# The first chunk's weight blocks of an MLP's down projection, placed and loaded in another order

## The chip, the core and the metric

The kernel runs on one core of a Trainium2 chip. The metric is the device time of one execution in microseconds (us); the time of a kernel is the median of its runs.

## The reference, cut to what matters

A trunk of two encoder layers on one sequence of 1024 rows of 1024 floats. Each layer mixes the rows (Fourier mixing, attention, a convolution), and then an MLP follows, whose second half is what the change touches:

```python
D_MODEL, SEQ, DEPTH, D_FF = 1024, 1024, 2, 4096
for l in range(DEPTH):
    ...                                        # token mixing, layer norm
    h = jnp.square(jax.nn.relu(x @ w_ff1[l]))  # 1024 x 4096
    x = layer_norm(ALPHA * x + h @ w_ff2[l], ln2_g[l], ln2_b[l])
```

## The kernel before

**Arithmetic.** All is float32. TensorE multiplies a float32 matrix as a high and a low part: `split` (lines 167 to 169) lets ScalarE (ACT) write the high part (L168) and VectorE (DVE) or GpSimd (POOL) the rest (L169), and `mm3` (L173 to L176) issues three matmuls, high by high (L174), high by low (L175) and low by high (L176). Both operands have to be split before.

**Seven products.** Both matrix products of the MLP are made by seven block products in place of eight (the scheme of Strassen and Winograd), so blocks of the weights and of the activations are added and subtracted before they are split. In `ff`, 16 pairs of columns of `w_ff1` go through the seven products one after the other, and the seven combinations of hidden activations that the second product needs go to DRAM as `h_scratch`.

**Down projection.** `ff_down` works through 4 chunks of the 4096 hidden columns, each with seven products in the order `DOWN = (1, 2, 6, 5, 3, 7, 4)`: 28 steps. Step i has one of three places for its operands: A, the activations, loaded from `h_scratch` and split by `down_a` (L1403 to L1410: ACT the high part, POOL and VectorE the low one), and W, the weights, split by `prepare2`. Places 0 and 2 have A in a tile `w` and W in `T`; place 1 has both in `T`. A chunk needs four 1 MB blocks of `w_ff2`, called 11, 12, 21 and 22. Product 1 takes block 11, product 2 block 21. Product 6, the third step, needs `d` = 22 - (12 - 11), made in two halves (tile `d`, one buffer, L1473), and product 5, the fourth, needs 12 - 11 (L1470). Products 3, 7 and 4 need 22, 22 - 12 and 21 - `d`.

**The start of the first chunk.** The last two of the 16 pairs load blocks 11 and 21 early into the freed row tiles `rw` (L1363 to L1367), and products 1 and 2 are split from there inside `ff` (L1382, L1388). Then `up.close()` gives these pools back, and `ff_down` loads the four blocks (11 and 21 for the second time) into four buffers of the tile `b`, in the order 11, 12, 22, 21 (L1451). Residual rows of x come through the four small tiles `raw` (`residual`, L1485).

**What sets the order.** The order on each engine is set by a scheduler when the program is built, which plays the program through with its own costs. Each engine runs its list in order. All DMAs are issued by SyncE (SP), one list, whose loads and stores go through one hardware queue (q1).

Of the kernel before, what the change touches and what calls it, by code (L numbers as in the profile page):

```python
# [15 lines left out]
F32 = mybir.dt.float32  # L16
F32R = mybir.dt.float32r
AF = mybir.ActivationFunctionType
OP = mybir.AluOpType
# [3 lines left out]
P = 128  # L23
S = 1024
D = 1024
NT = S // P
KT = D // P
# [22 lines left out]
PAIRS, CHUNK = DFF // (2 * P), 4  # L50
# [58 lines left out]
class Trunk:  # L109
# [879 lines left out]
    def ff(self, l, Wh, psum, last):  # L989
        nc, tc, a = self.nc, self.tc, self.a  # L990
        v, g, act = nc.vector, nc.gpsimd, nc.scalar
# [3 lines left out]
        w2 = a["w_ff2"][l].rearrange("(c j i p) (b n) -> c i b p j n", j=CHUNK, i=2, p=P, b=2)  # L995
# [3 lines left out]
        def operands():  # L999
            W = self.ws.tile([P, KT, 2, 256], F32R, tag="w", name="w", bufs=2)  # L1000
            return W.rearrange("p k i n -> p (k i n)").rearrange("p (q i n) -> p q i n", q=4, i=2)
# [9 lines left out]
        up = ExitStack()  # L1011
        E = up.enter_context(tc.tile_pool(name="sum", bufs=1, side="right", reuse_waits="tile"))
        E = E.tile([P, 3, 4, 2, 512], F32R, name="E")
        p1 = up.enter_context(tc.tile_pool(name="up", bufs=1, reuse_waits="tile"))

        B = {1: slots[0], 2: slots[2], 3: E[:, 0], 5: E[:, 1], 6: E[:, 2], 7: slots[1], 4: slots[3]}

        ahead = [{n: self.T[:, k + j, :, 0:512] for j, n in enumerate((1, 2))} for k in (2, 6)]

        def load_rows(pool, n):  # L1020
            rw = pool.tile([P, KT, 256], F32, tag="rw", name="rw", bufs=1)
            for h in range(0, KT, 4):
                self.dma(rw[:, h:h + 4], w1[:, h:h + 4, n * 256:(n + 1) * 256])
            return rw
# [5 lines left out]
        class Pair:  # L1030
            def __init__(me, pool, n):
                me.rw, me.ops = load_rows(pool, n), {}
# [51 lines left out]
        def product(o, n, ops, first):  # L1084
            for k in range(4):
                self.mm3(o, [ops[n][:, i, k * P:(k + 1) * P] for i in (0, 1)], [B[n][:, k, i] for i in (0, 1)],
                         first and k == 0, k == 3, True)
# [5 lines left out]
        with tc.tile_pool(name="zo", bufs=1, reuse_waits="tile") as zp:  # L1093
# [104 lines left out]
            def bank():  # L1198
                return acc.tile([P, 512], F32, tag="x", name="x", bufs=6)
# [23 lines left out]
        p2 = up.enter_context(tc.tile_pool(name="up2", bufs=1, reuse_waits="tile"))  # L1223
# [99 lines left out]
        coming = third.prepare()  # L1323
# [30 lines left out]
        for n in range(2, PAIRS):  # L1354
            final = n == PAIRS - 1
            if not final:
                following = Pair((p1, p2)[(n + 1) % 2], n + 1)
                coming = following.prepare()
            else:
                following, coming = None, iter(())  # L1360
                wa, wb = operands(), operands()
                places = [(wa, slots[0]), (slots[2], slots[1]), (wb, slots[3])]
            if n >= PAIRS - 2:  # L1363
                row = (p1, p2)[n % 2].tile([P, KT, 256], F32, tag="rw", name="rw", bufs=1)
                row = row.rearrange("p k n -> p (k n)").rearrange("p (j n) -> p j n", j=CHUNK)
                self.dma(row, w2[0, n - PAIRS + 2, 0])
                early = [row] if n == PAIRS - 2 else early + [row]  # L1367
            H, ops = Hidden(n), pair.ops
            X, Y, Z = bank(), bank(), bank()
            product(X, 1, ops, True)  # L1370
            H.done1(X)
            product(Y, 6, ops, True)
            H.done6(Y)
            product(Z, 5, ops, True)
            H.done5(Z)
            product(X, 2, ops, False)
            H.done2(X)
            next(coming, None)
            next(coming, None)
            if final:  # L1380
                self.down_a(places[0][0], 0, 1)
                self.split(places[0][1][:, :, 0], places[0][1][:, :, 1], early[0])  # L1382
            product(Y, 7, ops, False)
            H.done7(Y)
            next(coming, None)
            if final:
                self.down_a(places[1][0], 0, 2)
                self.split(places[1][1][:, :, 0], places[1][1][:, :, 1], early[1])  # L1388
            product(Z, 3, ops, False)
            H.done3(Z)  # L1390
            H.sums()
            next(coming, None)
            X = bank()
            product(X, 4, ops, True)
            H.done4(X)
            for _ in coming:
                pass
            pair = following
        up.close()
        return self.ff_down(l, places, w2, last)  # L1400


    def down_a(self, A, ch, n):  # L1403
# [7 lines left out]

    def ff_down(self, l, places, w2, last):
        nc, tc, a = self.nc, self.tc, self.a
        v, g, act = nc.vector, nc.gpsimd, nc.scalar
        keep = ExitStack()
# [3 lines left out]
        rows = [y.rearrange("p i n -> p (i n)") for y in x]  # L1421
# [15 lines left out]
        with ExitStack() as c:  # L1437
            acc = c.enter_context(tc.tile_pool(name="xq", bufs=1, space=PSUM, reuse_waits="tile"))
            p3 = c.enter_context(tc.tile_pool(name="down", bufs=1, reuse_waits="tile"))

            def quarter():
                q = p3.tile([P, 2, D], F32, tag="b", name="b", bufs=4)
                return q.rearrange("p i n -> p (i n)").rearrange("p (j n) -> p j n", j=CHUNK)

            def load(ch, *names):
                for k in names:
                    coming[k] = quarter()
                    self.dma(coming[k], w2[ch, k // 10 - 1, k % 10 - 1])

            blocks, coming = {}, {}  # L1450
            load(0, 11, 12, 22, 21)  # L1451
            blocks, coming = coming, {}
            R = {n: [p3.tile([P, 512], F32, name=f"r{n}{t}") for t in range(4)] for n in (1, 6, 5)}
            R.update({n: [x[t + h][:, j] for t in range(4)] for n, h, j in ((2, 0, 0), (3, 0, 1), (4, 4, 0), (7, 4, 1))})

            def sub(dst, x, y):
                v.tensor_tensor(dst, x, y, OP.subtract)  # L1457


            def prepare2(i):  # L1460
                nonlocal blocks, coming
                ch, n = i // 7, DOWN[i % 7]
                A, W = places[i % 3]
                self.down_a(A, ch, n)
                more = ch + 1 < PAIRS // CHUNK
                if n == 1:
                    load(ch, 22)
                    blocks, coming = coming, {}
                if n == 6:
                    sub(blocks[11], blocks[12], blocks[11])  # L1470
                    for h in (slice(0, 2), slice(2, 4)):
                        d = p3.tile([P, 2, 512], F32, tag="d", name="d", bufs=1)
                        sub(d, blocks[22][:, h], blocks[11][:, h])  # L1473
                        sub(blocks[21][:, h], blocks[21][:, h], d)
                        self.split(W[:, h, 0], W[:, h, 1], d)
                    return
                if n == 3 and more:
                    load(ch + 1, 11)
                if n == 7:
                    sub(blocks[12], blocks[22], blocks[12])  # L1480
                if n == 4 and more:
                    load(ch + 1, 21, 12)
                self.split(W[:, :, 0], W[:, :, 1], blocks[{1: 11, 2: 21, 5: 11, 3: 22, 7: 12, 4: 21}[n]])
# [5 lines left out]

            steps = 7 * PAIRS // CHUNK  # L1490
            prepare2(2)
            for i in range(steps):
                ch, n = i // 7, DOWN[i % 7]
                final = ch == steps // 7 - 1
                A, W = places[i % 3]
# [5 lines left out]
                for t in range(4):  # L1501
# [6 lines left out]
                    r = R[n][t]  # L1508
# [30 lines left out]
                if 3 <= i + 3 < steps:  # L1539
                    prepare2(i + 3)  # L1540
# [64 lines left out]
```

## Time and profile before

| | us |
|---|---|
| median of 3 runs | 2338.55 (2334.68 to 2340.46) |
| the profiled execution | 2349.58 |
| its span, first to last instruction | 2347.8 |
| TensorE busy | 2220.0 |
| VectorE busy | 1782.8 |
| ScalarE busy | 1076.9 |
| GpSimd busy | 792.8 |

Rows below come from the profiled execution; their times count from the start of the span. PE is TensorE, DVE VectorE, ACT ScalarE, POOL GpSimd, SPq the list of DMAs. In a timeline row the first number is the start, the second the duration, and what stands in square brackets is the engine's idle time before it and who ended it. The first layer's down projection starts at about 858 us, the second's at about 2014 us.

### The profile page before, as it was taken

The page shows a single profiled execution, that of the slowest core. Times are in us where ns is not written, and L with a number is a line of the kernel's source. Part 1 is how long each engine was busy: PE and PEld are TensorE (multiplying, and loading weights), DVE is VectorE, ACT ScalarE, POOL GpSimd, SP SyncE. Part 2 cuts the span into 40 slices and gives each one's busy share as a digit, 9 for nine tenths or more (in the row PEclk, how much of TensorE's full clock was granted, in tenths as well). Part 3 has the DMA queues.
Part 4 walks back from the last instruction along what each step waited for, and adds up shares of the span by engine and source line. Part 5 has one row for each costly group of instructions (what it writes and reads, how often), then busy time and mean ns, then how long its engine had stood idle before and what let it go on. Part 6 is the DMA issues. An engine that isn't in the chain of part 4 may idle for free. (4 is left out here: it accounts for less than half of the span.)

```text
span 2347.8 us, 31000 instructions
## 1 busy us (share of the span) xinstructions
PE 2220.0 (95%) x11212; PEld 1873.3 (80%) x11212; DVE 1782.8 (76%) x2494; ACT 1076.9 (46%) x1851; POOL 792.8 (34%) x540
## 2 busy tenths in 40 slices
PE   7999999998999999999989999999899999899997
PEld 6888887976777877888788898788678778688886
DVE  7687668978776757778957866787887777767699
ACT  3343767844333344333343447677443333434333
POOL 2361203016332333434514702110353323443353
PEclk9999999999999999999999999999999999999999
DMA  8444763043444476644223539621344444765433
GB/s 309 131 118 148 203 190 108 19 162 126 148 148 148 150 238 238 208 140 142 89 90 97 152 113 269 168 72 64 125 153 153 148 148 153 269 215 166 161 104 108
DMA packets 222854, 357.44 MB, mean 152 GB/s; under 512 B 21320, under 2 KB 100620, under 8 KB 221612
## 3 DMA queue, kind: packets, MB, share of 16 engines
q1 hardware_dynamic: 222700, 355.45, 46.7%
q8 instruction: 89, 1.46, 0.3%
q14 instruction: 65, 0.53, 0.1%
HBM read 244.44 MB, written 115.15 MB: 153 GB/s over the span
## 5 line engine op out<-in xcount | busy, mean ns | idle before, releaser
L174 PE MATMUL x<-T,w 128*128 128x512 f32 x1088 | 424.9, 393 | 21.1 <-ACT T L168 5.9
L175 PE MATMUL x<-T,w 128*128 128x512 f32 x1088 | 427.1, 393 | 7.5 <-DVE T L169 7.5
L176 PE MATMUL x<-T,w 128*128 128x512 f32 x1088 | 426.7, 393 | 5.2 <-POOL w L1409 2.6
L174 PEld LDWEIGHTS x<-T,w 128*128 128x128 f32 x1088 | 205.7, 189 | 69.4 <-issue 8.6
L175 PEld LDWEIGHTS x<-T,w 128*128 128x128 f32 x1088 | 206.6, 190 | 51.5 <-DVE T L169 8.6
L176 PEld LDWEIGHTS x<-T,w 128*128 128x128 f32 x1088 | 206.4, 190 | 50.3 <-POOL w L1409 4.1
L1409 POOL TENSOR_TENSOR w<-w 128x512 fp32r<-128x512 f32 x76 | 142.9, 1901 | 240.4 <-ACT w L1407 240.4
L169 POOL TENSOR_TENSOR w<-raw,w 128x512 fp32r<-128x512 f32 x96 | 138.0, 1462 | 239.2 <-ACT w L168 235.6
L169 POOL TENSOR_TENSOR w<-s,w 128x512 fp32r<-128x512 f32 x68 | 102.8, 1522 | 252.9 <-ACT w L168 199.6
L174 PE MATMUL x<-E,w 128*128 128x512 f32 x384 | 151.0, 393 | 4.6 <-ACT h L1266 4.6
L176 PE MATMUL x<-E,w 128*128 128x512 f32 x384 | 150.9, 394 | 2.0 <-POOL w L169 1.9
L175 PE MATMUL x<-E,w 128*128 128x512 f32 x384 | 150.6, 392 | 0.0
L174 PE MATMUL s<-w,T 128*128 128x256 f32 (+1 forms) x432 | 136.9, 318 | 7.4 <-ACT T L168 7.0
L168 ACT CAST T<-b 128x2048 fp32r<-128x2048 f32 x44 | 83.9, 1907 | 126.3 <-PE x L176 109.0
L169 DVE TENSOR_TENSOR T<-b,T 128x2048 fp32r<-128x2048 f32 x44 | 103.8, 2359 | 45.7 <-ACT T L168 45.7
L176 PE MATMUL s<-w,T 128*128 128x256 f32 (+1 forms) x432 | 135.5, 315 | 1.7 <-POOL T L169 1.2
L175 PE MATMUL s<-w,T 128*128 128x256 f32 (+1 forms) x432 | 135.1, 313 | 1.3 <-POOL w L169 1.3
L169 POOL TENSOR_TENSOR w<-rw,w 128x512 fp32r<-128x512 f32 x60 | 94.0, 1582 | 122.2 <-ACT w L168 122.2
L1044 DVE TENSOR_TENSOR s<-rw 128x512 f32<-128x512 f32 x62 | 52.1, 841 | 104.7 <-DMA rw<-in_w_ff_dram 101.0
L174 PE MATMUL x<-T 128*128 128x512 f32 x320 | 125.0, 391 | 0.0
L176 PE MATMUL x<-T 128*128 128x512 f32 x320 | 124.5, 389 | 0.0
L175 PE MATMUL x<-T 128*128 128x512 f32 x320 | 124.5, 389 | 0.0
(376 smaller groups left out, 5812.2 us busy)
## 6 DMA issues: line engine op xcount, KB each, us to landing
h_scratch<-h SPq DMA_DIRECT2D x224, 256.0 KB, 2.5
w<-h_scratch SPq DMA_DIRECT2D x38, 1024.0 KB, 5.4
rw<-in_w_ff_dram SPq DMA_DIRECT2D x64, 512.0 KB, 4.9
b<-in_w_ff_dram SPq DMA_DIRECT2D x32, 1024.0 KB, 6.2
raw<-x_scratch SPq DMA_DIRECT2D x72, 256.0 KB, 4.8
T<-h_scratch SPq DMA_DIRECT2D x18, 1024.0 KB, 5.2
raw<-in_w_in_dram SPq DMA_DIRECT2D x64, 256.0 KB, 3.4
x_scratch<-x SPq DMA_DIRECT2D x32, 256.0 KB, 6.2
```

The source lines that it names most:

```text
L168: self.nc.scalar.copy(hi, src)
L169: (lo_eng or self.nc.vector).tensor_tensor(lo, src, hi.bitcast(F32), OP.subtract)
L174: mm(out, l[0], r[0], start=first, stop=False, skip_group_check=more)
L175: mm(out, l[0], r[1], start=False, stop=False, skip_group_check=more)
L176: mm(out, l[1], r[0], start=False, stop=last, skip_group_check=more)
L1044: eng.tensor_tensor(quad(out), x, y, op)
L1409: nc.gpsimd.tensor_tensor(A[:, j, 1], f32[:, j], A[:, j, 0].bitcast(F32), OP.subtract)
```

## The change

The change keeps block 11 where it was loaded early: the tile `rw` moves to a pool of its own, `p0`, which stays open through `ff_down`. Within the last pair, once block 11 has been split for product 1, block 12 is loaded in four pieces of 256 KB through the tiles `raw`, and VectorE subtracts in place, so that the tile then holds 12 - 11. `ff_down` loads three blocks in place of four, in the order 22, 12, 21, into three buffers of `b`; in the later chunks block 11 goes to `p0`'s tile. In product 6 the split of `d` is written ahead of the subtraction 21 - `d`.

```diff
+        keep = ExitStack()
+        p0 = keep.enter_context(tc.tile_pool(name="rows", bufs=1, reuse_waits="tile"))
...
-            rw = pool.tile([P, KT, 256], F32, tag="rw", name="rw", bufs=1)
+            rw = (p0 if pool is p1 else pool).tile([P, KT, 256], F32, tag="rw", name="rw", bufs=1)
...
-                row = (p1, p2)[n % 2].tile([P, KT, 256], F32, tag="rw", name="rw", bufs=1)
+                row = (p0, p2)[n % 2].tile([P, KT, 256], F32, tag="rw", name="rw", bufs=1)
...
             H.done3(Z)
             H.sums()
+            if final:
+
+                b11 = early[0]
+                for j in range(CHUNK):
+                    r = self.raw().rearrange("p a n -> p (a n)")
+                    self.dma(r, w2[0, 0, 1, :, j])
+                    v.tensor_tensor(b11[:, j], r, b11[:, j], OP.subtract)
...
-            def quarter():
-                q = p3.tile([P, 2, D], F32, tag="b", name="b", bufs=4)
+            def quarter(k):
+                if k == 11:
+                    q = p0.tile([P, KT, 256], F32, tag="rw", name="rw", bufs=1).rearrange("p k n -> p (k n)")
+                    return q.rearrange("p (j n) -> p j n", j=CHUNK)
+                q = p3.tile([P, 2, D], F32, tag="b", name="b", bufs=3)
...
-            load(0, 11, 12, 22, 21)
-            blocks, coming = coming, {}
+            load(0, 22, 12, 21)
+            blocks, coming = {**coming, 11: b11}, {}
...
                 if n == 6:
-                    sub(blocks[11], blocks[12], blocks[11])
+                    if ch:
+                        sub(blocks[11], blocks[12], blocks[11])
                     for h in (slice(0, 2), slice(2, 4)):
                         d = p3.tile([P, 2, 512], F32, tag="d", name="d", bufs=1)
                         sub(d, blocks[22][:, h], blocks[11][:, h])
+                        self.split(W[:, h, 0], W[:, h, 1], d)
                         sub(blocks[21][:, h], blocks[21][:, h], d)
-                        self.split(W[:, h, 0], W[:, h, 1], d)
```

The scheduler puts the four pieces of block 12 near the start of the MLP, as soon as the `raw` tiles are free; before, the residual rows of the first four tiles stood there. On SP's list, from the load of product 1's activations to the blocks, before:

```order
L141 DMA w<-h_scratch 128x4x512
L141 DMA T<-h_scratch 128x4x512
L141 DMA h_scratch<-h 128x512
L141 DMA gb<-in_ln_g_dram 128x1024
L141 DMA h_scratch<-h 128x512
L141 DMA gb<-in_ln_b_dram 128x1024
L141 DMA w<-h_scratch 128x4x512
L141 DMA h_scratch<-h 128x512 x5
L141 DMA b<-in_w_ff_dram 128x4x512 x4
```

and after:

```order
L141 DMA w<-h_scratch 128x4x512
L141 DMA raw<-x_scratch 128x512 x4
L141 DMA T<-h_scratch 128x4x512
L141 DMA h_scratch<-h 128x512
L141 DMA gb<-in_ln_g_dram 128x1024
L141 DMA h_scratch<-h 128x512
L141 DMA gb<-in_ln_b_dram 128x1024
L141 DMA w<-h_scratch 128x4x512
L141 DMA h_scratch<-h 128x512 x5
L141 DMA b<-in_w_ff_dram 128x4x512 x3
```

Four loads of residual rows (256 KB each) now stand ahead of `T`, the activations of product 2, and three blocks stand where four stood.

On VectorE, for product 6 of the first chunk, before (`b_7826` is block 11, `b_7828` 12, `b_7830` 22, `d_7852` the first half of `d`, `T` the operand that is split):

```order
L1457 TENSOR_TENSOR b_7826<-b_7828,b_7826 128x2048
L1510 SCALAR_TENSOR_TENSOR x0_7802<-raw_7938,x_7925 128x512
L1510 SCALAR_TENSOR_TENSOR x1_7803<-raw_7954,x_7941 128x512
L1457 TENSOR_TENSOR d_7852<-b_7830,b_7826 128x1024
L1457 TENSOR_TENSOR b_7828<-b_7830,b_7828 128x2048
L169 TENSOR_TENSOR T_64<-b_7826,T_64 128x4x512
L1510 SCALAR_TENSOR_TENSOR x2_7804<-raw_7970,x_7957 128x512
L169 TENSOR_TENSOR T_64<-d_7852,T_64 128x2x512
```

and after (`rw_7513` holds 12 - 11, `b_7841` is 22, `b_7843` 12, `b_7845` 21):

```order
L1471 TENSOR_TENSOR d_7864<-b_7841,rw_7513 128x1024
L169 TENSOR_TENSOR T_64<-rw_7513,T_64 128x4x512
L1471 TENSOR_TENSOR b_7843<-b_7841,b_7843 128x2048
L1525 SCALAR_TENSOR_TENSOR x0_7817<-raw_7950,x_7937 128x512
L169 TENSOR_TENSOR T_64<-d_7864,T_64 128x2x512
L1525 SCALAR_TENSOR_TENSOR x1_7818<-raw_7966,x_7953 128x512
L1471 TENSOR_TENSOR b_7845<-b_7845,d_7864 128x1024
L1525 SCALAR_TENSOR_TENSOR x2_7819<-raw_7982,x_7969 128x512
L1525 SCALAR_TENSOR_TENSOR x3_7820<-raw_7998,x_7985 128x512
L1421 TENSOR_TENSOR w_7659<-w_7659 128x2x512
L1471 TENSOR_TENSOR d_7869<-b_7841,rw_7513 128x1024
```

The row of seven instructions up to the low part of `d`'s first half has become one of four ahead of it; the subtraction 12 - 11 is gone from here.

## Rows read from the trace of the kernel before

**Rows 1.** The page: busy time, share of the span and instructions of each engine.

```profile
PE 2220.0 (95%) x11212; PEld 1873.3 (80%) x11212; DVE 1782.8 (76%) x2494; ACT 1076.9 (46%) x1851; POOL 792.8 (34%) x540
```

**Rows 2.** Busy time by stretch: PE, PEld, DVE, ACT, POOL, granted clock, DMA, GB/s.

```profile
857.00:866.00 9.00, 7.12 (x23) 5.12 (x23) 7.94 (x8) 5.67 (x5) 7.22 (x4) 0.81 0.55 171
...
884.00:898.00 14.00, 8.13 (x26) 5.94 (x25) 14.00 (x10) 7.67 (x5) 7.00 (x3) 0.76 0.70 249
898.00:930.00 32.00, 32.00 (x143) 26.51 (x142) 19.64 (x15) 15.08 (x14) 9.47 (x6) 1.00 0.71 243
...
2038.00:2054.00 16.00, 8.50 (x23) 6.01 (x22) 16.00 (x12) 8.54 (x5) 7.45 (x4) 0.68 0.69 248
```

**Rows 3.** TensorE's waits on GpSimd, 855 to 900 us: total, times, longest.

```profile
PE x L176 <- POOL w L1409: 1.9, 2, 1.2
```

**Rows 4.** TensorE's timeline in the first layer, 884 to 897 us.

```profile
884.16 0.39 PE L176 MATMUL x<-T 128*128 128x512 f32 x1
886.55 1.20 PE L174 MATMUL x<-T,w 128*128 128x512 f32 x4 [2.00 <-ACT T L168]
891.61 0.80 PE L175 MATMUL x<-T,w 128*128 128x512 f32 x1 [3.87 <-DVE T L169]
...
896.55 0.39 PE L174 MATMUL x<-T,w 128*128 128x512 f32 x1
```

**Rows 5.** The same in the second layer, 2037 to 2054 us.

```profile
2037.95 0.39 PE L176 MATMUL x<-T 128*128 128x512 f32 x1
2042.22 1.44 PE L174 MATMUL x<-T,w 128*128 128x512 f32 x4 [3.87 <-ACT T L168]
2047.28 0.80 PE L175 MATMUL x<-T,w 128*128 128x512 f32 x1 [3.63 <-DVE T L169]
...
2053.57 0.39 PE L175 MATMUL x<-T,w 128*128 128x512 f32 x1
```

**Rows 6.** VectorE's timeline in the first layer, 880 to 902 us.

```profile
880.79 2.29 DVE L1457 TENSOR_TENSOR b<-b 128x2048 f32<-128x2048 f32 x1 [6.42 <-DMA b<-in_w_ff_dram]
...
889.74 0.68 DVE L1510 SCALAR_TENSOR_TENSOR x<-raw,x 128x512 f32<-128x512 f32 x1
890.33 1.22 DVE L169 TENSOR_TENSOR T<-d,T 128x1024 fp32r<-128x1024 f32 x1
...
899.22 2.30 DVE L1457 TENSOR_TENSOR d<-b 128x1024 f32<-128x1024 f32 x1
```

**Rows 7.** VectorE's timeline in the second layer, at the same place.

```profile
2036.46 2.29 DVE L1457 TENSOR_TENSOR b<-b 128x2048 f32<-128x2048 f32 x1 [7.64 <-DMA b<-in_w_ff_dram]
```

**Rows 8.** The four blocks, first layer: SP's timeline; time to landing (tile view).

```profile
871.87 2.96 SPq L141 DMA_DIRECT2D b<-in_w_ff_dram  x4
...
DMA to landing us min/median/max: 6.2/8.2/10.1
```

**Rows 9.** Issue of the activations of products 1 and 2, first layer.

```profile
847.94 0.37 SPq L141 DMA_DIRECT2D w<-h_scratch  x1
852.02 0.37 SPq L141 DMA_DIRECT2D T<-h_scratch  x1
```

**Rows 10.** ScalarE's high parts of activations, products 1 and 5, first layer.

```profile
856.04 1.91 ACT L1407 CAST w<-w 128x2048 fp32r<-128x2048 f32 x1 [7.51 <-DMA w<-h_scratch]
...
888.97 1.90 ACT L1407 CAST w<-w 128x2048 fp32r<-128x2048 f32 x1 [0.67 <-DMA w<-h_scratch]
```

**Rows 11.** GpSimd's low parts of activations, products 1, 2 and 5, first layer.

```profile
858.03 4.00 POOL L1409 TENSOR_TENSOR w<-w 128x512 fp32r<-128x512 f32 x2 [16.11 <-ACT w L1407]
862.78 5.49 POOL L1409 TENSOR_TENSOR T<-T 128x512 fp32r<-128x512 f32 x2 [0.75 <-ACT T L1407]
...
890.94 3.97 POOL L1409 TENSOR_TENSOR w<-w 128x512 fp32r<-128x512 f32 x2 [14.16 <-ACT w L1407]
```

**Rows 12.** VectorE before product 1's low part, first layer.

```profile
857.99 1.23 DVE L1410 TENSOR_TENSOR w<-w 128x1024 fp32r<-128x1024 f32 x1 [8.87 <-ACT w L1407]
```

**Rows 13.** Busy time, 848.5 to 852.5 us; columns as in rows 2.

```profile
848.50:852.50 4.00, 4.00 (x19) 3.31 (x18) 0.62 (x2) 0.04 (x1) 0.00 (x0) 1.00 1.06 395
```

More of the change, by code (lines that the diff above doesn't have):

```diff
@@ L1399, in ff @@
         up.close()
-        return self.ff_down(l, places, w2, last)
+        with keep:
+            return self.ff_down(l, places, w2, last, p0, b11)
     def down_a(self, A, ch, n):
@@ L1410, in down_a, with ff_down @@
         nc.vector.tensor_tensor(A[:, 2:4, 1], f32[:, 2:4], A[:, 2:4, 0].bitcast(F32), OP.subtract)
-    def ff_down(self, l, places, w2, last):
+    def ff_down(self, l, places, w2, last, p0, b11):
         nc, tc, a = self.nc, self.tc, self.a
@@ L1446, in load @@
                 for k in names:
-                    coming[k] = quarter()
+                    coming[k] = quarter(k)
                     self.dma(coming[k], w2[ch, k // 10 - 1, k % 10 - 1])
             blocks, coming = {}, {}
-            load(0, 11, 12, 22, 21)
-            blocks, coming = coming, {}
+            load(0, 22, 12, 21)
+            blocks, coming = {**coming, 11: b11}, {}
             R = {n: [p3.tile([P, 512], F32, name=f"r{n}{t}") for t in range(4)] for n in (1, 6, 5)}
```

## The prediction

> **What bounds the kernel now.** The page comes first: TensorE is busy for 2220.0 of 2347.8 us [rows 1], so only time in which TensorE stands still or runs slowly can be won. The busy time by stretch then shows where that is. In 898 to 930 us it starts 143 matmuls in 32 us, one in 0.224 us, at a granted clock of 1.00 (2.4 GHz). In 884 to 898 us it is busy for 8.13 of 14 us at a granted clock of 0.76, and in the second layer, 2038 to 2054 us, for 8.50 of 16 us at 0.68 [rows 2]. Both stretches are the start of product 6 in the first chunk, and the change works there.
>
> TensorE's timeline names the waits. In the first layer the last matmul of product 2 starts at 884.16, so the next could start at 884.4. It starts at 886.55, held by ScalarE's high part of `d`; four matmuls later it stands again until 891.61, held by VectorE's low part, and then runs 12 steps in 4.94 us, nearly twice as long as they should take [rows 4]. From 884.4 to 896.55 it has done 16 steps, 3.6 us at full rate, so 8.6 us are lost. In the second layer it is free at 2038.2 and has done 19 steps (4.3 us) by 2053.57: 11.1 us lost [rows 5]. **The two stalls together are 19.7 us**, and no more than that can come from them.
>
> The chain behind each wait is on VectorE. It waits 6.42 us for block 12, subtracts at 880.79, takes residual rows in, makes `d`, subtracts 22 - 12, splits product 5's weights, and only then, at 890.33, makes the low part of `d` [rows 6]. The second layer begins the same chain at 2036.46 [rows 7].
>
> **What the change removes and moves.** (1) *The blocks.* The four are issued from 871.87 on. The first lands 6.2 us later, at 878.1 [rows 8], the second at 880.8, where the subtraction starts [rows 6]: one block in 2.7 us, so a third at 883.5. The change puts 22 first and 12 second, and 12 - 11 is there already. So `d` can start at 878.1 in the first layer and at 2036.46 - 2.7 = 2033.8 in the second.
>
> (2) *VectorE up to the low part of `d`.* By the new row: `d` 1.2 (as the split of the same size at 890.33), the split of 12 - 11 2.3 and 22 - 12 2.3 (as the subtraction at 880.79), one residual 0.7, the low part of `d` 1.2 [rows 6]. First layer: 878.1 + 1.2 + 2.3 = 881.6, block 12 is there, 883.9, 884.6, 885.8. TensorE, free at 884.4, does three matmuls that need the high part alone, until 885.1, and waits 0.7 us. ScalarE's high part, 1 us behind `d`, is long done. Second layer: 2033.8 + 3.5 = 2037.3, then 2039.6, 2040.3, 2041.5; TensorE is there at 2038.9 and waits 2.6 us.
>
> (3) *VectorE up to the second half of `d`.* Behind that stand 1 residual (0.7), 21 - `d` (1.2), 2 residuals (1.4), the low part of product 5's activations, `d`'s second half, the split of 22, 21 - `d` and the split of `d`. The last five are 1.2 + 1.2 + 2.3 + 1.2 + 1.2 = 7.1 us if GpSimd is quiet, and 11.5 to 12 us if it is not: the same subtraction took 2.30 us at 899.22 [rows 6], beside GpSimd. So the low part of the second half is done 10.4 to 15.3 us after TensorE started again. TensorE has 21 + 24 + 4 matmuls until then, 11.0 us, so it waits 0 to 4.3 us. GpSimd works for 4 us on product 5's activations and later for 5.5 us on the next [rows 11], which leaves a gap between; I take 1.3 us in each layer.
>
> (4) *Product 5's activations* land behind three blocks, not four: 2.7 us before 888.97 [rows 10], 886.3. ScalarE needs 1.9 and GpSimd 4.0 us [rows 10, 11], so the two tiles that GpSimd makes are ready at 892.2. TensorE wants the second at 885.8 + 28 steps = 892.1. No wait, but nothing to spare.
>
> (5) *The clock.* In 857 to 866 us two waits of 1.9 us in all [rows 3] went with a granted clock of 0.81; 23 matmuls ran where 40 fit [rows 2], 3.8 us lost, so 1.9 beside the waits. For the 2.6 us of the second layer I charge the same 1.9 us (0 to 2.9, what that layer loses so now: 15 steps in 6.29 us, [rows 5]); for 0.7 us in the first nothing (0 to 1.9).
>
> (6) *Added.* Four subtractions of 128x512, 0.7 us each by the nearest row, stand on VectorE before product 1's low part, where it is idle for 8.87 us [rows 12]: nothing, as long as that part waits for ScalarE. The pieces of block 12 are loaded at the start of the MLP and have been there for hundreds of us. The four residual loads (1 MB) that stood there now leave at 850 to 852, as VectorE frees `raw`, on SP behind the load of product 1's activations (847.94) and ahead of `T` (852.02) [rows 9]. The queue is full there, DMA share 1.06 [rows 13], so `T` lands up to 2.7 us later. Its low part is made until 868.3 [rows 11] and product 2 starts 48 matmuls before 884.4, at 873.6: 5 us cover it. By 866 the share has fallen to 0.55 on average [rows 2], so the queue has caught up before the blocks. One block less (1 MB) and the second load of 11 go away.
>
> **The sum.** Left in the first layer: 0.7 + 1.3 = 2.0 of 8.6 us; in the second: 2.6 + 1.9 + 1.3 = 5.8 of 11.1. Won: 6.6 + 5.3 = 11.9 us. Against the profiled execution, 2349.6 us, that is 2337.7; the runs shown have their median 11 us lower, at 2338.55, and the stalls are the same program's, so 2338.55 - 11.9 = **2326.7**. With the bounds of (3) and (5) the win is 2.9 us (0.7 + 4.3 + 1.9 and 2.6 + 4.3 + 2.9 left) to 16.4 us (0.7 and 2.6 left).
>
> **The rivals.** *A: the stall only moves to the second half of `d`.* VectorE's row is a chain without a gap, and every subtraction in it that meets GpSimd takes twice as long: the bound of 2.9 us, 2335.6. For it speaks the 2.30 us row; against it that GpSimd is idle between its two jobs. The Trainium skill, "SBUF — State Buffer", Who interferes with whom, says that a VectorE instruction with two SBUF inputs contends with a GpSimd instruction that reads SBUF. The trace agrees (1.22 against 2.30 us for the same form).
>
> *B: the residual loads delay product 1.* If the DMA engines take the 1 MB in turns with product 1's activations, in flight from 847.94, these land 2.7 us after 856.04 [rows 10]; ScalarE, GpSimd (idle 16.11 us for it, [rows 11]) and TensorE all wait for that. Price: 2.7 us in both layers and 1.9 us of clock in the second, 7.3 us: 2334.0. Against it: the blocks landed one after the other, 2.7 us apart, which is a queue worked off in order. The Trainium skill, "DMA: Bandwidth & Descriptors", Queues, rings and completion order, says that completion is not first in, first out for one issuing engine. By that page B could happen; the landings of this trace show order. The same price holds if the queue has not caught up and the blocks come 2.7 us later.
>
> *C: slower.* In the buffer ring of three, the next chunk's block 12 takes the buffer of block 12, which is free only when product 7's weights are split; on SP's list product 4's activations stand behind this load. Products 3 and 7 give 96 matmuls, 21.5 us, of cover; two loads (5.4 us), landing, ScalarE and GpSimd (1.9 + 4.0) take some 13, so 8.5 us are to spare. If SP stood there for 20 us, each layer would lose 11.5 us: 23 - 11.9 = 11 us slower, 2349.6. It turns to slower from about 14.5 us on. Against it: product 7's split needs only product 6's last matmul, and that lies before the end of product 5 in the new row.
>
> *D: it does not do what it says*, the blocks or pieces not being where they should; the lists above exclude it, but for the 2.7 us counted under B.
>
> **How the numbers follow.** Forecast 0.68, A 0.14, B and D 0.12, C 0.04, and 0.02 for a gain above the bound. A measurement can tell some 0.3%, 7 us, from no change. The forecast's cases lie mostly above that (6 to 16 us), A and B below it: faster 0.67, same 0.28, slower 0.05. The range reaches from the best bound, 16.4 us, with 2 us for the spread of the runs (2334.68 to 2340.46), to A: 2320 to 2336.
>
> **What would show it.** In the profile after, block 22 should be subtracted at about 878 us, 6.2 us behind its issue; TensorE's waits at product 6 should be below 1 and 3 us, with the granted clock of that stretch near 1.00 in the first layer; a wait on VectorE's `T` some 11 us later tests (3); product 1's cast should still start at about 856 us, or B holds; and no wait may appear at product 4. The forecast is wrong if the second half's wait passes 3 us in both layers, or if the blocks land later behind the moved residual loads.

## The result and the profile after

The changed kernel takes 2328.55 us (median of 16 runs, 2322.37 to 2334.08), the kernel before beside it 2340.03 us (16 runs). The ratio is 0.9949, 95% interval 0.9937 to 0.9960: 12 us or half a per cent faster. The forecast was 2326.7 us.

The profiled execution has a span of 2326.3 us, 21.5 us less than the one before. That is more than the medians differ by, because the execution profiled before was 9.5 us above its median; the last paragraph on the prediction comes back to what of that is spread.

TensorE is busy nearly as long as it was (2217.1 us, 2220.0 before, [rows 1]), so that what changed is its idle time and its clock. First the busy times by engine, of the page:

```profile
PE 2217.1 (95%) x11212; PEld 1869.2 (80%) x11212; DVE 1776.1 (76%) x2500; ACT 1077.1 (46%) x1851; POOL 793.3 (34%) x540
```

The busy time by stretch (length; busy us and instructions of PE, PEld, DVE, ACT, POOL; granted clock; DMA share; GB/s) answers to [rows 2]: product 1 and the start of product 6 in the first layer, then the start of product 6 in the second.

```profile
853.00:862.00 9.00, 8.28 (x36) 6.34 (x35) 7.02 (x6) 6.71 (x5) 4.43 (x3) 1.00 0.95 330
880.00:886.00 6.00, 4.14 (x11) 2.74 (x10) 6.00 (x8) 2.52 (x2) 0.54 (x1) 0.72 0.75 241
...
2024.00:2042.00 18.00, 14.82 (x62) 11.32 (x62) 17.99 (x13) 8.23 (x7) 7.27 (x4) 1.00 0.79 274
```

The stretch in which TensorE stands or runs slowly was 12 us long in the first layer (884.4 to 896.55, [rows 4]) and is now 6 us. In the second layer the 18 us at the start of product 6 hold 62 matmuls at a granted clock of 1.00, where 16 us held 23 at 0.68.

TensorE's timeline, first layer, then second (start, duration, instruction; in brackets the idle time before it and who ended it), answers to [rows 4, 5]:

```profile
879.78 0.61 PE L174 MATMUL x<-T,w 128*128 128x512 f32 x2
881.63 0.50 PE L174 MATMUL x<-T,w 128*128 128x512 f32 x1 [1.23 <-DVE x L1525]
882.77 0.79 PE L175 MATMUL x<-T,w 128*128 128x512 f32 x1 [0.63 <-DVE T L169]
883.36 0.63 PE L176 MATMUL x<-T,w 128*128 128x512 f32 x1
...
885.92 0.49 PE L174 MATMUL x<-T,w 128*128 128x512 f32 x1
...
895.68 0.50 PE L175 MATMUL x<-T,w 128*128 128x512 f32 x1
...
2024.06 0.61 PE L174 MATMUL x<-T,w 128*128 128x512 f32 x2
2025.74 0.50 PE L174 MATMUL x<-T,w 128*128 128x512 f32 x1 [1.06 <-DVE x L1525]
2026.88 0.50 PE L175 MATMUL x<-T,w 128*128 128x512 f32 x1 [0.63 <-DVE T L169]
...
2039.82 0.50 PE L175 MATMUL x<-T,w 128*128 128x512 f32 x1 [1.49 <-DVE T L169]
```

The two waits of 2.0 and 3.87 us, and of 3.87 and 3.63 us, have become small ones: two in the first layer, three in the second. The wait for the low part of `d` (the one on `T`) is 0.63 us in both layers. Ahead of it stands a wait that the prediction doesn't have: the third L174 needs a buffer of the tile `x` (there are six of them in PSUM, the memory that takes TensorE's sums), and that one is freed when VectorE has added the first residual of product 2 (L1525, the sum x0). Behind it the two layers differ: in the first TensorE runs seven steps at half rate and finds the second half of `d` ready at 895.68, in the second it runs at full rate and waits 1.49 us for that half at 2039.82.

VectorE's timeline of the first layer answers to [rows 6]:

```profile
875.35 1.23 DVE L1471 TENSOR_TENSOR d<-b,rw 128x1024 f32<-128x1024 f32 x1 [3.67 <-DMA b<-in_w_ff_dram]
876.49 2.29 DVE L169 TENSOR_TENSOR T<-rw,T 128x2048 fp32r<-128x2048 f32 x1
878.69 2.29 DVE L1471 TENSOR_TENSOR b<-b 128x2048 f32<-128x2048 f32 x1
880.89 0.68 DVE L1525 SCALAR_TENSOR_TENSOR x<-raw,x 128x512 f32<-128x512 f32 x1
881.49 1.22 DVE L169 TENSOR_TENSOR T<-d,T 128x1024 fp32r<-128x1024 f32 x1
...
887.75 2.30 DVE L1471 TENSOR_TENSOR d<-b,rw 128x1024 f32<-128x1024 f32 x1
889.98 2.28 DVE L169 TENSOR_TENSOR T<-b,T 128x2048 fp32r<-128x2048 f32 x1
892.18 1.21 DVE L1471 TENSOR_TENSOR b<-b,d 128x1024 f32<-128x1024 f32 x1
893.32 2.31 DVE L169 TENSOR_TENSOR T<-d,T 128x1024 fp32r<-128x1024 f32 x1
```

`d` now needs one landing, block 22's, 6.3 us behind the issue at 869.03, and starts the row; before, it stood behind 12 - 11. The subtraction 22 - 12 (878.69, 2.29 us) stands ahead of the residual that frees the buffer and of the low part of `d`. The latter is ready 7.4 us behind block 22's landing, the low part of the second half (893.32 + 2.31) 20.3 us behind it.

**A measure for the runs.** In the table "lost" is the sum, over TensorE's starts from the end of product 2 until it runs at full rate in the second half of product 6, of what each step (from one start to the next) takes beyond 0.227 us: waits, slow steps, and the first step behind a wait, which takes 0.34 us. "Lost at product 1" is the same for the stall that [rows 3] show. For the kernels with the change, the sums in the expectations of the runs are 0.2 to 1.1 us lower; most of that is this last part.

### The profile page after: what moved, and what is told of

Its sections match the earlier page's. It is cut to its first block, busy times and chain, and to the rows that moved or that the text cites. A ratio compares the mean times of both kernels' runs of the same rounds, so it can differ in the third digit from the quotient of the medians.

```text
span 2326.3 us, 31019 instructions
## 1 busy us (share of the span) xinstructions
PE 2217.1 (95%) x11212; PEld 1869.2 (80%) x11212; DVE 1776.1 (76%) x2500; ACT 1077.1 (46%) x1851; POOL 793.3 (34%) x540
## 5 line engine op out<-in xcount | busy, mean ns | idle before, releaser
L174 PE MATMUL x<-T,w 128*128 128x512 f32 x1088 | 425.5, 393 | 12.2 <-DVE x L1441 4.7
L174 PEld LDWEIGHTS x<-T,w 128*128 128x128 f32 x1088 | 205.3, 189 | 60.8 <-issue 9.7
L174 PE MATMUL x<-E,w 128*128 128x512 f32 x384 | 150.6, 392 | 5.9 <-ACT h L1269 4.5
L174 PE MATMUL s<-w,T 128*128 128x256 f32 (+1 forms) x432 | 137.0, 318 | 5.8 <-ACT T L168 5.4
L1418 ACT CAST w<-w 128x2048 fp32r<-128x2048 f32 x38 | 72.7, 1912 | 129.4 <-DMA w<-h_scratch 122.4
L174 PE MATMUL x<-T 128*128 128x512 f32 x320 | 126.1, 394 | 0.0
L456 DVE SCALAR_TENSOR_TENSOR o<-hp,cvT,o 128x1024 f32<-128x1024 f32 x88 | 113.3, 1287 | 2.4
```

Of the source, the lines that this page charges most:

```text
L174: mm(out, l[0], r[0], start=first, stop=False, skip_group_check=more)
L456: v.scalar_tensor_tensor(o, hp[:, m, k:k + S], cvT[:, m, k:k + 1], o, OP.mult, OP.add)
L1418: nc.scalar.copy(A[:, :, 0], f32)
```

## The experiments

Ten executions were profiled, two of them of the two kernels themselves. "Less" is the ratio's distance from 1, times 2342 us.

| kernel | lost at product 1, us (layers 1, 2) | lost at product 6, us (layers 1, 2; sum before rounding) | ratio, interval | less, us |
|---|---|---|---|---|
| before | 4.0, 1.1 | 8.5, 11.1; 19.6 | 1 | |
| before with the last hunk alone | 1.3, 0.9 | 9.9, 11.0; 20.9 | 1.0000 (0.9988 to 1.0013) | 0 |
| changed | 1.1, 1.3 | 4.2, 4.1; 8.3 | 0.9949 (0.9937 to 0.9960) | 11.9 |
| changed, again | 2.9, 1.5 | 4.0, 4.2; 8.1 | 0.9945 (0.9927 to 0.9964) | 12.9 |
| no pieces, 12 first | 1.3, 1.1 | 7.0, 6.4; 13.4 | 0.9971 (0.9956 to 0.9985) | 6.8 |
| pieces, 12 first | 1.3, 1.2 | 7.5, 5.3; 12.8 | 0.9964 (0.9951 to 0.9976) | 8.4 |
| residual loads behind `T` | 1.4, 1.1 | 6.4, 3.9; 10.3 | 0.9967 (0.9952 to 0.9982) | 7.7 |
| 22 - 12 late | 1.7, 1.6 | 3.9, 4.0; 7.9 | 0.9925 (0.9904 to 0.9946) | 17.6 |
| 22 - 12 and two splits late | 1.4, 1.5 | 1.9, 2.5; 4.4 | 0.9933 (0.9910 to 0.9956) | 15.7 |
| the same, again | 1.8, 1.7 | 2.3, 1.6; 3.9 | 0.9928 (0.9909 to 0.9948) | 16.9 |

With 20.2 us lost before (the mean of the first two rows), the loss at product 6 alone gives 11.9, 12.1, 6.8, 7.4, 9.9, 12.3, 15.8 and 16.3 us less from the third row on. All but one lie in their ratio's interval; that of "22 - 12 late" falls 0.3 us short of it, and the two profiles of before differ by more (19.6 and 20.9 us). So the time goes where product 6's stalls go.

### The changed kernel again

No edit.

> The changed kernel once more, as a second profile and as the measure for the runs beside it. Theory: the waits at product 6 are set by VectorE's row, so they repeat within 0.3 us: 1.1 to 1.2 us on x0 and 0.6 us on T in both layers, and 1.5 us on the second half of d in the second layer; the ratio is 0.995 again. What differed between the profiles at product 1 (1.9 us of waits before, 0.7 after) is then the spread of one execution: it may be anywhere from 0.7 to 1.9 us here. Rival: the change itself wins there, by the pieces that moved residual loads and T; then product 1's waits are 0.7 us again. Which layer loses the clock is expected to be the same by the rival that waits alone set it (0.89 in the first layer, 1.00 in the second), and free to change by the theory that it hangs on more than these waits.

Measured: 0.9945, and product 6 loses 8.1 us. TensorE's waits in the first layer:

```profile
856.17 0.50 PE L176 MATMUL x<-T,w 128*128 128x512 f32 x1 [1.56 <-POOL w L1420]
857.86 0.50 PE L176 MATMUL x<-T,w 128*128 128x512 f32 x1 [0.73 <-POOL w L1420]
880.18 0.50 PE L174 MATMUL x<-T,w 128*128 128x512 f32 x1 [0.94 <-DVE x L1525]
881.32 0.50 PE L175 MATMUL x<-T,w 128*128 128x512 f32 x1 [0.63 <-DVE T L169]
894.24 0.50 PE L175 MATMUL x<-T,w 128*128 128x512 f32 x1 [1.49 <-DVE T L169]
```

Two things are settled here. The waits at product 1 are 2.3 us, above the 1.9 us of before, with the change in place: the 0.7 us of the first profile was not won by the change. And this time the first layer keeps its full clock and waits 1.49 us for the second half instead. From the step behind the first wait on `T` to the step on the second half it is 12.91 us in the first profile (882.77 to 895.68, with seven slow steps), 12.92 us here (881.32 to 894.24) and 12.94 us in the second layer (2026.88 to 2039.82), both without: VectorE's row sets that distance, and the slow clock only used up a wait that would have come anyway. The rival that the waits alone decide on the clock falls at product 1: 2.3 us of waits there have no slow step behind them here, and 1.9 us had seven in the kernel before [rows 2, 3].

### The last hunk alone

In the kernel before, only the last part (hunk) of the diff is made: the split of `d` is written ahead of 21 - `d`, nothing else.

```diff
+                        self.split(W[:, h, 0], W[:, h, 1], d)
                         sub(blocks[21][:, h], blocks[21][:, h], d)
-                        self.split(W[:, h, 0], W[:, h, 1], d)
```

> The kernel before with only the last part of the change: the split of d is written ahead of the subtraction 21 - d. The instructions of all engines stand in the same order as before, since the scheduler had put them so already. Theory: ratio 1.000 within the interval, product 6 loses 8.5 us in the first layer and 11.1 us in the second as before; its profile is so a second one of the kernel before. What it tells apart is the stall at product 1 of the first layer, where the profile of before lost 3.8 us: if that is the spread of one execution (three profiles of kernels with the change lost 0.9, 2.6 and 1.4 us there), it is anywhere from 0.9 to 3.8 us here. Rival: the kernel before always loses 3.8 us there, because its T and w are queued in another way, and the change wins 1 to 3 us at product 1 as well; then it is 3.5 us or more here. A second rival, that the last part brings a gain by itself, expects 1 to 2 us less than before.

Measured: 1.0000. This part of the change does nothing by itself, so the profile is a second one of the kernel before. TensorE's waits, first layer, then second, and the issue of the four blocks in the first:

```profile
855.95 0.50 PE L176 MATMUL x<-T,w 128*128 128x512 f32 x1 [0.73 <-POOL w L1409]
...
880.70 2.08 PE L174 MATMUL x<-T,w 128*128 128x512 f32 x4 [3.81 <-ACT T L168]
885.76 0.80 PE L175 MATMUL x<-T,w 128*128 128x512 f32 x1 [2.98 <-DVE T L169]
...
2028.36 1.23 PE L174 MATMUL x<-T,w 128*128 128x512 f32 x4 [3.71 <-ACT T L168]
2033.42 0.80 PE L175 MATMUL x<-T,w 128*128 128x512 f32 x1 [3.83 <-DVE T L169]
...
865.73 3.02 SPq L141 DMA_DIRECT2D b<-in_w_ff_dram  x4
```

At product 1 it loses 1.3 us where the first profile of before lost 4.0 [rows 2, 3]: that stall is the spread of an execution, and the rival that the change wins there falls. It also explains why the first layer of before lost 1.4 us less at product 6 than here (8.5 against 9.9). From the issue of the blocks to the end of product 2 it is 12.5 us there (871.87 to 884.4, [rows 4, 8]) and 11.0 us here (865.73 to 876.7). Waits at product 1 don't change that distance: in the changed kernel's second profile, with 2.3 us of them, it is 11.0 us as well. The seven slow steps behind the waits, which no other profile has at this place, held up TensorE and not the blocks.

### Without the pieces

12 - 11 is subtracted where it was, after 12 has landed, and 12 is loaded first.

```diff
-                for j in range(CHUNK):
-                    r = self.raw().rearrange("p a n -> p (a n)")
-                    self.dma(r, w2[0, 0, 1, :, j])
-                    v.tensor_tensor(b11[:, j], r, b11[:, j], OP.subtract)
...
-            load(0, 22, 12, 21)
+            load(0, 12, 22, 21)
...
-                    if ch:
-                        sub(blocks[11], blocks[12], blocks[11])
+                    sub(blocks[11], blocks[12], blocks[11])
```

> The changed kernel without its pieces: the first block stays in its early place, but 12 - 11 is subtracted when 12 has landed, so 12 comes first, 22 second, 21 third, and the residual loads and T are as before. Theory: d starts when both 12 - 11 and 22 are there, so 2.7 us later than in the changed kernel and 2.7 us earlier than before, and VectorE has 12 - 11 (2.3 us) in its row: the wait at product 6 is 3.3 to 5 us in the first layer and 5 to 7 in the second, half the gain stays: 4 to 7 us below the kernel before, ratio 0.997 to 0.998. Rival: the order of need alone makes the gain (22 no longer third); then it is within 1 us of the changed kernel, ratio 0.995.

Measured: 0.9971, 13.4 us lost; half the gain stays. VectorE's timeline, first layer:

```profile
875.67 2.29 DVE L1467 TENSOR_TENSOR rw<-b,rw 128x2048 f32<-128x2048 f32 x1 [3.88 <-DMA b<-in_w_ff_dram]
878.44 1.23 DVE L1467 TENSOR_TENSOR d<-b,rw 128x1024 f32<-128x1024 f32 x1 [0.48 <-DMA b<-in_w_ff_dram]
...
884.58 1.22 DVE L169 TENSOR_TENSOR T<-d,T 128x1024 fp32r<-128x1024 f32 x1
```

`d` starts 2.8 us behind the first landing, since it needs the second, and the low part is ready 10.1 us behind the first landing against 7.4 us in the changed kernel. The rival, that the order of need alone makes the gain, falls.

### Pieces, but 12 first

```diff
-            load(0, 22, 12, 21)
+            load(0, 12, 22, 21)
```

> The changed kernel with blocks 12 and 22 loaded in the other order, 12 first; the pieces are kept. Theory: d needs 22, which lands as the second, 2.7 us later, while 12 - 11 is split already when it lands. So d starts 2.7 us later than in the changed kernel and T 0.4 us later than that without the 2.3 us of the split between: product 6 loses 2 to 4 us more in the two layers together than the 7.5 to 7.8 us of the changed kernel, ratio to the kernel before 0.995 to 0.997. It stays 2 to 4 us ahead of the kernel without pieces (13.2 us lost, 12 first as well), which is the 2.3 us subtraction in VectorE's row. Rival: the landing of the blocks doesn't matter because VectorE's row is the only limit; then the loss is that of the changed kernel within 0.5 us. Second rival: the order of the loads is what the pieces' gain rests on; then it loses 13 us as the kernel without pieces.

Measured: 0.9964, 12.8 us lost. The theory expected 2 to 4 us more than the changed kernel loses (8.1 and 8.3) and falls; the second rival, a loss as without the pieces (13.4), holds by the number. VectorE's timeline, first layer:

```profile
872.83 2.29 DVE L169 TENSOR_TENSOR T<-rw,T 128x2048 fp32r<-128x2048 f32 x1 [2.52 <-ACT T L168]
876.35 1.23 DVE L1471 TENSOR_TENSOR d<-b,rw 128x1024 f32<-128x1024 f32 x1 [1.23 <-DMA b<-in_w_ff_dram]
...
880.89 1.22 DVE L1471 TENSOR_TENSOR b<-b,d 128x1024 f32<-128x1024 f32 x1
882.03 1.22 DVE L169 TENSOR_TENSOR T<-d,T 128x1024 fp32r<-128x1024 f32 x1
```

What I had overlooked is in the rows of the kernel without pieces: there the subtraction 12 - 11 (875.67 to 877.96) ran in the gap between the two landings, and VectorE still waited 0.48 us for block 22. With 12 first, the pieces take away work from a time in which VectorE waits anyway. The split of 12 - 11 moves into that gap in its place (872.83), but the scheduler fills part of the room behind `d`: 21 - `d` (880.89), 1.2 us, stands ahead of the low part here and behind it in the changed kernel. So the pieces are worth 5 us of the 12 together with block 22 landing first and little without it; how the 5 us divide between the landing and this other order on VectorE is not shown.

### Residual loads behind T

The four residual loads of product 2 are held on SyncE until `T` is issued (`self.second` is that load).

```diff
...
+                with self.tc.issue_after(self.second.ins) if t < 4 and half == 0 else nullcontext():
-                    self.dma(r, self.xs[t * P:(t + 1) * P, half * 512:half * 512 + 512])
+                    self.dma(r, self.xs[t * P:(t + 1) * P, half * 512:half * 512 + 512])
```

> The changed kernel with the four residual loads of product 2 held on SyncE until T's load is issued, so that they no longer stand between product 1's activations and T. The scheduler puts VectorE's low part of d ahead of 22 - 12 here as well, as in the kernel with the late 22 - 12, so it is compared with that one (6.8 us lost at product 6, 0.9925). Rival B says that the residual loads delay product 1's activations by 2.7 us; then their landing behind the issue falls from 6.9 to 7.2 us (second layer) to some 4.3 us, and product 1's stall of 0.9 to 1.3 us goes. Theory: they queue behind these activations and delay them by 0.4 us at most; the landing is 6.7 to 6.8 us as in the kernel without pieces, the stall at product 1 is 0.9 us, and the ratio is 0.992 to 0.995.

The second layer is read for what the residual loads do to product 1; in the first the times lie from 6.8 to 8.5 us over all profiles and do not tell the kernels with them from those without (7.3 and 7.2 us on the mean). SyncE's issues and ScalarE's cast of product 1's activations, of the changed kernel:

```profile
1990.31 0.37 SPq L141 DMA_DIRECT2D w<-h_scratch  x1
1992.10 2.16 SPq L141 DMA_DIRECT2D raw<-x_scratch  x4
1994.39 0.37 SPq L141 DMA_DIRECT2D T<-h_scratch  x1
...
1997.24 1.91 ACT L1418 CAST w<-w 128x2048 fp32r<-128x2048 f32 x1 [6.34 <-DMA w<-h_scratch]
```

and of this one:

```profile
1996.99 0.37 SPq L1416 DMA_DIRECT2D w<-h_scratch  x1
2001.07 0.37 SPq L1416 DMA_DIRECT2D T<-h_scratch  x1
2001.54 2.10 SPq L141 DMA_DIRECT2D raw<-x_scratch  x4
2003.69 1.91 ACT L1420 CAST w<-w 128x2048 fp32r<-128x2048 f32 x1 [6.10 <-DMA w<-h_scratch]
```

From the issue to the cast it is 6.93 us with the residual loads right behind the activations and 6.70 us without. In the other profiles' second layers it is 6.86, 7.16, 7.20, 7.18 and 7.32 us with them (12 first; changed again; 22 - 12 late; both runs with two splits late), and 6.49, 6.73 and 6.77 us without (last hunk; before; no pieces): 7.1 against 6.7 on the mean. The residual loads cost product 1's activations 0.4 us in this layer, not the 2.7 us of rival B, and it falls. In the second layer the stall at product 1 is 1.1 us here and 0.9 to 1.1 us in the other kernels without them, against 1.2 to 1.7 us with them.

The time was expected lower: the ratio is 0.9967, above that of the changed kernel and of the kernel with 22 - 12 late, whose VectorE row it has as far as the residuals. Product 6 loses 2.4 us more than in the latter, all of it in the first layer (6.4 against 3.9 us): 1.6 us in slow steps, and most of the rest because block 22 landed 7.1 us behind its issue (870.40 to 877.48), where the changed kernel has 6.3. Whether the later residual loads or one execution's spread did that stays open.

### 22 - 12 late

The subtraction is held on VectorE until the low part of the first half of `d` is made.

```diff
-                        self.split(W[:, h, 0], W[:, h, 1], d)
+                        act.copy(W[:, h, 0], d)
+                        low = v.tensor_tensor(W[:, h, 1], d, W[:, h, 0].bitcast(F32), OP.subtract)
+                        if ch == 0 and h.start == 0:
+                            self.low = low
...
-                    sub(blocks[12], blocks[22], blocks[12])
+                    with self.tc.issue_after(self.low.ins) if ch == 0 else nullcontext():
+                        sub(blocks[12], blocks[22], blocks[12])
```

> The changed kernel with 22 - 12 of the first chunk made behind the low part of d's first half instead of ahead of x0. Theory: the two waits of the first half (1.1 and 0.6 us in each layer) were the 2.3 us of that subtraction, so they go; but it is only put 2 places later, so the low part of d's second half comes at the same time, while TensorE comes 2.3 us earlier: the wait there grows from 0 and 1.5 us to 0.5 to 2 and 3 to 4 us. Sum: 0 to 4 us less than the changed kernel (only the slow clock of the first layer and what the second half has to spare are won), ratio to the kernel before 0.993 to 0.995. Rival: 22 - 12 isn't what holds x0 (x0 waits for product 2's end); then the waits of the first half stay at 1.1 and 0.6 us and the ratio is 0.995.

TensorE's waits at product 6 in the first layer:

```profile
884.50 0.50 PE L176 MATMUL x<-T,w 128*128 128x512 f32 x1 [0.32 <-POOL w L1420]
886.71 0.50 PE L176 MATMUL x<-T,w 128*128 128x512 f32 x1 [0.78 <-POOL w L1420]
893.35 0.50 PE L175 MATMUL x<-T,w 128*128 128x512 f32 x1 [1.54 <-DVE T L1490]
```

Measured: 0.9925, 7.9 us lost. The first half's waits on x0 and on `T` are gone, so it was this subtraction that caused them. But only 0.2 to 0.4 us are won at product 6 against the changed kernel (the ratio says 5 us; its interval reaches down to 12.6 us less than before, and the changed kernel has 11.9 and 12.9): the low part of the second half is ready 20.3 us behind block 22's landing as before (873.01 to 893.30), and on the way there TensorE now waits 1.1 us for GpSimd's half of product 5's activations, which the changed kernel reached without a wait. I had expected the whole shift at the second half, 3 to 4 us in the second layer, and nothing on GpSimd; there it was 1.58 us.

### 22 - 12 and two splits late

22 - 12, and with it the splits of 22 and 12 for products 3 and 7, wait for the low part of the second half of `d`; the scheduler then also puts TensorE's first four matmuls of that half 17 places earlier.

```diff
+                behind = lambda: self.tc.issue_after(self.low.ins) if ch == 0 and n in (3, 7) else nullcontext()
                 if n == 7:
-                    sub(blocks[12], blocks[22], blocks[12])
+                    with behind():
+                        sub(blocks[12], blocks[22], blocks[12])
...
-                self.split(W[:, :, 0], W[:, :, 1], blocks[{1: 11, 2: 21, 5: 11, 3: 22, 7: 12, 4: 21}[n]])
+                with behind():
+                    self.split(W[:, :, 0], W[:, :, 1], blocks[{1: 11, 2: 21, 5: 11, 3: 22, 7: 12, 4: 21}[n]])
```

(with the split of `d` written out as in the kernel above, for both halves).

> The changed kernel with 22 - 12 of the first chunk, and with it the splits of 22 and 12 (products 3 and 7), made behind the low part of d's second half: VectorE's row then holds between block 22's landing and that part only what product 6 and 21 - d need. Theory: all waits of product 6 but one of below 0.5 us go, in both halves and both layers, and with them the slow clock: of the 4.0 us that each layer still loses there 3 are won, 5 to 7 us less than the changed kernel, ratio to the kernel before 0.992 to 0.993. Products 5 and 3 keep TensorE busy for 96 matmuls, so that 22 - 12 and the two splits (7 us) are hidden. Rival: the order on VectorE is not the limit, but the landing of 22; then the first wait stays, as a wait on T or on ScalarE's high part, and the gain is below 2 us. Slower by 2 us or more would mean that product 3's or 7's weights come late.

> The kernel with 22 - 12 and the splits of 22 and 12 behind the low part of d's second half, once more, for a narrower interval and a second profile. Theory: product 6 loses 3.5 us in both layers together again, 16 us less than before, ratio 0.9932; what is left are 0.2 to 0.8 us on d's first half (block 22's landing) and 0.3 us each on ScalarE's high part of d and GpSimd's low part of product 5's activations. Rival: its waits move from execution to execution as those of product 1 do; then the sum is anywhere from 2 to 7 us.

Measured: 0.9933 and 0.9928; 4.4 and 3.9 us lost. VectorE's row in the first layer (of the first of the two):

```profile
877.69 1.23 DVE L1471 TENSOR_TENSOR d<-b,rw 128x1024 f32<-128x1024 f32 x1 [3.79 <-DMA b<-in_w_ff_dram]
...
885.10 1.22 DVE L1471 TENSOR_TENSOR d<-b,rw 128x1024 f32<-128x1024 f32 x1
...
890.14 2.30 DVE L1490 TENSOR_TENSOR T<-d,T 128x1024 fp32r<-128x1024 f32 x1
892.37 2.28 DVE L1471 TENSOR_TENSOR b<-b 128x2048 f32<-128x2048 f32 x1
```

and TensorE's waits there:

```profile
882.90 0.50 PE L175 MATMUL x<-T,w 128*128 128x512 f32 x1 [0.17 <-DVE T L1490]
888.78 1.43 PE L174 MATMUL x<-T,w 128*128 128x512 f32 x5 [0.36 <-ACT T L1489]
891.42 0.50 PE L176 MATMUL x<-T,w 128*128 128x512 f32 x1 [0.30 <-POOL w L1420]
```

The low part of the second half comes 14.8 us behind the landing, not 20.3, and no step runs slowly in either layer. The rest is the landing of block 22 (0 to 0.8 us on `T`), ScalarE and GpSimd, 0.3 to 0.4 us each. So VectorE's order was what the changed kernel still lost there; the new order on TensorE was not needed for it, since at the old place the step on the low part would come 49 steps, 11.1 us, behind 882.90, at 894.0, and the part is ready at 892.4. Of all the kernels this one loses least at product 6, 3.8 to 4.4 us less than the changed kernel. The ratios say the same (0.9933 and 0.9928 against 0.9949 and 0.9945), but their intervals overlap, so that its lead over the changed kernel is shown by the rows and only made likely by the times. The times don't tell it from the kernel with 22 - 12 alone late (0.9925); all three are faster than the kernel before, with whole intervals below 1.

## Why the prediction was right

The mechanism was right: 7.8 us were forecast to be left at product 6, and 8.3 and 8.1 us are left; 11.9 us were to be won, the ratio says 11.9. That the sum came out so close is luck: two terms were off and cancelled, one in each layer (2.0 us forecast and 4.2 found in the first, 5.8 and 4.1 in the second).

- *The blocks, part (1).* Right. `d` starts at the first landing, 6.3 us behind the issue; the kernel without pieces shows 2.8 us from the first landing to the second.
- *The low part of `d`, part (2).* The row is right (7.7 us from landing to the end, 7.4 measured), the wait is not, in the first layer: 0.7 us forecast, 2.3 us found (1.39 at the buffer of `x` and 0.91 at `T`, both counted beyond 0.227 us). Most of the difference is an execution's spread taken for a property: TensorE's arrival at 884.4, 12.5 us behind the blocks' issue, was read from a profile with seven slow steps at product 1; in every other layer profiled it is 10.8 to 11.0 us. In the second layer 2.6 us were forecast and 2.1 found. The buffer that waits for x0 was not foreseen, but x0 and the low part stand in the same row next to each other, so it changes the name of the wait and not its end.
- *The second half, part (3).* Right in size. It is 12.9 us from TensorE's step behind the first low part to the step on the second, and the 49 steps up to there take 11.1 us: 1.8 us are lost, of which the profile shows 1.49 as a wait; 1.3 was taken, from 0 to 4.3. (By these bounds the smallest win is 3.0 us, not 2.9.)
- *The clock, part (5).* Here the step failed. 1.9 us were added for slow steps in the second layer, beside the second half's wait. The runs show one or the other, 1.8 us of those 12.9 each, since the low part of the second half is ready at the same time either way. Each layer therefore loses 4.0 to 4.2 us. That the clock fell in the first layer and not in the second was foreseen the other way round; the second profile has it fall in neither. So two of the signs that the prediction named did not come in the first layer: waits below 1 us (1.9 came) and a granted clock near 1.00 (0.72 in 880 to 886 us).
- *Product 5's activations, part (4).* Right, "no wait, but nothing to spare": none in the changed kernel, 1.1 us as soon as TensorE came 2 us earlier.
- *The pieces, part (6).* Right as to their price. VectorE made the four subtractions in 2.48 us at 847.28 and then still waited 5.14 us for ScalarE. The residual loads that moved cost product 1's activations 0.4 us in the second layer, within the spread of its stall.
- *The rivals.* A falls, the second half's wait is 1.5 us and not 4. B falls by the landings above. C falls: no wait appears at product 4. D falls: `d` starts 6.3 us behind the issue of its block.

Of the 21.5 us between the two profiled spans 11.3 are product 6, 2.9 product 1 in the first layer, which is spread, and the remaining 7 lie outside these stretches. That much is spread as well: between the issues of product 1's activations in the two layers, less what is lost at products 1 and 6 in between, the kernel before takes 1144.2 us (847.94 to 2004.62, less 12.5) and the same program in the profile of the last hunk 1137.0 us (842.95 to 1991.16, less 11.2).

## What to carry to other kernels

When several blocks must arrive before a chain can start, let the one that completes its first operation land first, and prepare everything that doesn't need it beforehand; preparation was worth little here (0.6 us less lost, both with 12 first) where the order of arrival left its engine waiting at that time anyway. Behind a removed stall, read the whole row of the engine that fed it: what stands between its landing and its two deadlines is the next stall. And before a stall goes into a sum by its measured length, ask for a second profile: one of the two stalls read here was the spread of one execution.

## What the runs showed of the hardware

- Waits of nearly the same size had different clocks behind them. 1.23 and 0.63 us of waiting on TensorE were followed by seven steps at the lower level (1.2 GHz, 0.42 us a step instead of 0.227) in one execution, and 0.94 and 0.63 us by none in another of the same kernel, nor 1.06 and 0.63 us in the second layer. At product 1 the longer waits, 2.3 us, had no slow step behind them, and the shorter, 1.9 us [rows 3], had seven. The Trainium skill, "TensorE: Matmul & The Clock Gate", What's actually happening, says of the start of a kernel that the number of slow matmuls differs between runs of the same one; these executions agree, in the middle of a kernel. A forecast can give such a cost bounds, not a value.
- A lower clock need not cost anything: 1.6 us of slow steps took the place of a 1.49 us wait behind them.
- Four residual loads, 1 MB together, issued on the same queue 1.8 us behind another 1 MB load made that one 0.4 us later on the mean in the second layer (7.1 against 6.7 us from issue to use; in the first no difference shows), where blocks of 1 MB landed 2.7 to 2.8 us apart. The Trainium skill, "DMA: Bandwidth & Descriptors", Queues, rings and completion order, says that completion is not first in, first out for one issuing engine. Here the order held but for this small delay: the activations were cast from 1997.24, and the residual rows, issued from 1992.10, took 5.7 us or more to land.
- VectorE's subtraction for the second half of `d` took 2.30 us in the changed kernel and 1.22 us in the one with two splits late, where it ended before GpSimd began at 887.86. In the changed kernel it started at 887.75, and GpSimd was at work from 885.46 to 888.98. So here 1.1 us on the chain depended on when the subtraction ran, not on what it does.
